# Second-layer logits on half of the array's rows for each of two heads, and output projections by 512 columns

## The chip, the cores and the metric

One core of one Trainium2 chip runs the whole kernel. Its engines are TensorE (PE in the profile, with PEld for its weight loads), VectorE (DVE), ScalarE (ACT), GpSimd (POOL) and SyncE (SP, which issues most DMAs). The metric is the device time of one execution in microseconds (us), as the median of several runs.

## The reference

A decoder trunk of two layers on a sequence of 1024 tokens with width 1024, in float32. Layer A is a gated DeltaNet layer; layer B is sliding-window attention with 32 query heads of 64 and four shared key and value heads. Both end with a projection by a weight of 2048 x 1024 that is added to the residual stream. The part that matters here:

```python
def swa_sink_mixer(h, w_in, q_gain, sinks, w_out, k_band, v_band, bias, mask):
    q, z = jnp.split(h @ w_in, 2, axis=-1)
    q = rms_norm(q.reshape(B, T, B_Q_HEADS, B_HD), q_gain) * (B_HD ** -0.5)
    q = q.reshape(B, nb, BLOCK, B_KV_HEADS, B_GROUP, B_HD)
    logits = jnp.einsum("bnqkgd,bnskd->bnkgqs", q, k_band).astype(jnp.float32) + bias
    ...
    o = jnp.einsum("bnkgqs,bnskd->bnqkgd", probs.astype(v_band.dtype), v_band)
    o = o.reshape(B, T, B_W) * jax.nn.silu(z)
    return o @ w_out          # and x = x + that, as at the end of layer A
```

A block is 128 queries, and its keys are the 128 of its own block and the 128 before them, so that each head's logits of a block are a 128 x 256 product over a depth of 64.

## The kernel before

Large products are taken at float32 precision by splitting each operand into a high part (rounded to the type fp32r, which TensorE takes in one pass) and a low part (the rest, again fp32r), and adding high x high, low x high and high x low in PSUM. Weights come in tiles of 128 x 1024 numbers: SP loads `wraw`, POOL or ACT makes `whi`, DVE makes `wlo` in two halves (`weight`, lines 138 to 158). TensorE's order is written out by hand: the code yields after small steps, and `interleave` lets a front stream of work go ahead by the numbers yielded while a back stream fills in. The other engines' instructions are put in order by a scheduler at build time.

*Output projections* (`out_proj`, called once for layer A with its weight `a_w_out` and once at the end for layer B with `b_w_out`). For each half of the tokens (512) and each half of the output columns (512), four PSUM banks `ps[c]`, one for each 128 tokens, collect 2048 rows of depth. `og_load` brings the layer's output in from HBM in four parts `k4` of 512 rows and splits them into `oh`, `ol`. A weight tile is 512 rows x 256 columns (`four` in `weights`): the loop over `b` takes the left and the right 256 columns, and each tile serves 4 x 4 x 3 = 48 matmuls with 256 moving columns. There are 32 such tiles in each projection, 3072 matmuls in both. The matmuls are lines 919 (`whi`, `oh`), 920 (`wlo`, `oh`) and 921 (`whi`, `ol`); line 925 adds the residual.

*Attention of layer B.* Eight groups of four heads (`groups`), eight blocks each: 64 blocks run through `b_attend`. For a block:

- `q_up` (lines 1137, 1139): POOL rounds the normalised queries to fp32r into `qh`, and DVE writes the low part beside it, so that a head has 64 high and 64 low numbers.
- `q_turn` (1146, 1149): TensorE transposes the four heads (fp32r, 128 x 128 each) into a PSUM tile `tp`, and ACT copies it to `qT`. Each head then fills all 128 rows of the array: high part above, low part below.
- `logits` (1166, 1167): for each head one matmul with the high keys `kh` and one with the low keys `kl`, 256 moving columns each. Both key tiles hold the 64 key rows twice, one above the other (`key_stack`). So a block has eight matmuls, four to each of two PSUM tiles `lg`. DVE then applies the mask (1168), adds the bias and takes the row maximum (1172); ACT does the exponentials (1182); POOL divides (1186).
- `turn` (1192): TensorE transposes the four heads' probabilities (float32), and ACT and DVE copy them out.
- `values` (1213): probabilities times values, two heads side by side on the left and right 64 columns of the array.

In each step of the loop of `b_attend` the calls are `turn(i)`, `q_turn(i + 3)` and `q_up(i + 4)`, `logits(i + 2)`, `values(i - 1)`, and between them the back stream computes the next queries (`gemm_tc`, lines 971 to 973, 256 columns) and gates (`gemm_ct`, lines 180, 182, 184, 512 columns).

Of the kernel before, what the change touches and what calls it, by code (L numbers as in the profile page):

```python
# [7 lines left out]
F32 = mybir.dt.float32  # L8
F32R = mybir.dt.float32r
# [9 lines left out]
P = 128  # L19
# [45 lines left out]
class Kernel:  # L65
# [831 lines left out]
    def out_proj(self, og, resid, cur, tiles, raws, px, acc, dst, finish):  # L897


        nc = self.nc  # L900
        for half in range(2):
            xs, nxt = [], []
            for cp in range(2):
                cs = slice(cp * 512, cp * 512 + 512)
                ps = [acc.tile([P, 2, 256], F32, name="acc") for _ in range(4)]
                for k4 in range(4):
                    oh, ol = cur[k4]
                    for b in range(2):
                        hi, lo = self.take()
                        if cp == 0 and (k4, b) == (2, 0):  # L910
                            self.flush()
                            for c in range(4):
                                xs.append(px.tile([P, D], F32, name="xo", bufs=4))
                                nc.sync.dma_start(xs[c], resid[half * 4 + c])
                        for c in range(4):
                            ts = slice(c * P, c * P + P)
                            po = ps[c][:, b, :]
                            for kk in range(4):
                                nc.tensor.matmul(po, oh[:, kk, ts], hi[:, kk, :], start=(k4 + kk + b == 0), stop=False)  # L919
                                nc.tensor.matmul(po, oh[:, kk, ts], lo[:, kk, :], start=False, stop=False)  # L920
                                nc.tensor.matmul(po, ol[:, kk, ts], hi[:, kk, :], start=False, stop=(k4 + kk + b == 7))  # L921
                                if kk % 2:
                                    self.tick()
                            if (k4, b) == (3, 1):
                                nc.vector.tensor_tensor(out=xs[c][:, cs], in0=ps[c].rearrange("p b c -> p (b c)"),
                                                        in1=xs[c][:, cs], op=ALU.add)
# [199 lines left out]
    def b_attend(self, groups):  # L1126

        nc, bp, sb, aps = self.nc, self.bp, self.sb, self.aps
        blocks = [(X, n) for X in groups for n in range(NB)]
        qh, qT, Ls, pTs = {}, {}, {}, {}  # L1130
# [11 lines left out]
        def q_turn(i):  # L1142
            t = qh.pop(i)
            ps = aps.tile([P, 4, P], F32R, name="tp", bufs=3)
            for e in range(4):
                nc.tensor.transpose(out=ps[:, e, :], in_=t[:, e, :, :].rearrange("p a d -> p (a d)"),
                                    identity=self.identr)
            qT[i] = bp.tile([P, 4, P], F32R, name="qT")
            nc.scalar.copy(out=qT[i], in_=self.f32(ps))

        def logits(i):

            X, n = blocks[i]
            kh, kl = X.keys
            sk = self.sink[:, 4 * X.hg:4 * X.hg + 4]
            q = qT.pop(i)
            k0 = 0 if n else P
            ksl = slice((n - 1) * P + k0, (n + 1) * P)
            L = Ls[i] = bp.tile([P, 4, P], F32, name="lsb", bufs=3)
            m = sb.tile([P, 4], F32, name="m")  # L1160
            two = [P, 2, P]
            for pr in range(2):
                ps = aps.tile([P, 2, 256], F32, name="lg")
                for j in range(2):
                    e = 2 * pr + j
                    nc.tensor.matmul(ps[:, j, k0:256], q[:, e, :], kh[:, ksl], start=True, stop=False)
                    nc.tensor.matmul(ps[:, j, k0:256], q[:, e, :], kl[:, ksl], start=False, stop=True)  # L1167
                nc.vector.copy_predicated(ps[:, :, P:256], self.up.bitcast(I32).unsqueeze(1).broadcast_to(two),
                                          ps[:, :, 0:P] if n else self.neg.unsqueeze(2).broadcast_to(two))
                for j in range(2):  # L1170
                    e = 2 * pr + j
                    nc.vector.tensor_tensor_reduce(out=L[:, e, :], in0=ps[:, j, P:256], in1=X.bias[:, e, :],
                                                   scale=1.0, scalar=sk[:, e:e + 1], op0=ALU.add, op1=ALU.max,
                                                   accum_out=m[:, e:e + 1])
            nm = sb.tile([P, 4], F32, name="nm")
# [41 lines left out]
                self.b_done(X)  # L1217

        last = len(blocks) - 1
        q_up(0)  # L1220
        q_up(1)
        q_turn(0)
        yield 1.0
        logits(0)
        q_turn(1)
        q_up(2)
        yield 1.5
        logits(1)
        q_turn(2)
        q_up(3)  # L1230
        yield 2.5
        fill = (1.2, 1.2, 0.6, 0.6, 1.2)
        steps = iter(())
        for i, (X, n) in enumerate(blocks):
            turn(i)
            yield fill[0]
            if i + 3 <= last:
                q_turn(i + 3)
            if i + 4 <= last:
                q_up(i + 4)  # L1240
            yield fill[1]
            if i + 2 <= last:
                logits(i + 2)
            yield fill[2]
            if X.hg < 7:
                nxt = groups[X.hg + 1]
                if n == 0:
                    nxt.keys, steps = self.key_stack(nxt.hg // 2) if X.hg % 2 else (X.keys, iter(()))
                    self.b_bias(nxt)
                next(steps, None)  # L1250
            yield fill[3]
            if i:
                values(i - 1)
            yield fill[4]
# [85 lines left out]
    def weights(self):  # L1340
# [15 lines left out]
                for b in (32 + 2 * i, 33 + 2 * i):  # L1356
                    yield col(self.win, b, None)
        for _ in range(2):
            for c in (0, 2):
                for k in range(4):  # L1360
                    for b in range(2):
                        yield four(rows("a_w_out"), k, c + b, None)
        wkv = I["w_kv"].rearrange("(k p) c -> p k c", p=P)
        for c in range(2):
            for k in range(2):
# [5 lines left out]
            else:  # L1371
                yield col(bin_, 16 + 2 * hg + j, self.gcolb[:, 8:16])
        for _ in range(2):
            for c in (0, 2):
                for k in range(4):
                    for b in range(2):
                        yield four(rows("b_w_out"), k, c + b, None)

    def dump(self, name, ap):
        self.nc.sync.dma_start(self.dbg[name], ap)  # L1380
# [21 lines left out]
```

## Time and profile before

| | us |
|---|---|
| median of 3 runs (1887.74 to 1893.08) | 1890.71 |
| the profiled execution | 1894.54 |
| its span, first to last instruction | 1892.8 |
| layer A up to its projection | 0 to 899.4 |
| layer A's projection (`out_proj`) | 899.4 to 1089.5 |
| keys, values, first queries | 1089.5 to 1167 |
| attention of layer B | 1167 to 1704.3 |
| layer B's projection (`out_proj`) | 1704.3 to 1892.8 |

TensorE is busy for 97% of the span, DVE for 65%, ACT for 44%, POOL for 27%. A matmul's duration in the profile is its latency from start to end; several are in the array at a time, so that the distance from one start to the next, not the duration, is what a matmul costs. A timeline row that ends in x8 stands for eight instructions of one line in a row; its duration runs from the first start to the last end.

### The profile page before, as it was taken

How to read it: one execution, taken by the hardware profiler on the slowest of the kernel's cores; microseconds unless marked ns; L12 is line 12 of the kernel's file. 1: busy time of each engine (PE TensorE's matmuls, PEld its weight loads, DVE VectorE, ACT ScalarE, POOL GpSimd, SP SyncE). 2: the span in 40 equal slices, each digit the busy share in tenths (PEclk: the TensorE clock that was granted, in tenths of full speed). 3: DMA queues.
4: the chain of work that ended last, by engine and by line, in shares of the span. 5: the costliest groups of instructions: out<-in, count | busy, mean ns of one | idle time of the engine just before them, and what ended most of it. 6: DMA issues, size and time to landing. Idle time of an engine off the chain costs nothing.

```text
span 1892.8 us, 34012 instructions
## 1 busy us (share of the span) xinstructions
PE 1829.7 (97%) x13186; PEld 1567.2 (83%) x13186; DVE 1239.6 (65%) x3014; ACT 838.1 (44%) x1968; POOL 512.6 (27%) x581
## 2 busy tenths in 40 slices
PE   6999999999999998999999999999999999999999
PEld 5667777787878776778999999888788788879999
DVE  6677776868595878765545366787776776753432
ACT  6446353635445364423011043656756666771100
POOL 0222222322232223221211232333433333321211
PEclk9999999999999999999999999999999999999999
DMA  4611111111111111133654321111211111226542
GB/s 149 143 37 34 56 45 57 34 56 46 34 57 34 46 34 58 33 96 99 229 182 152 112 90 46 42 38 46 67 32 48 56 49 43 73 73 200 188 166 82
DMA packets 151270, 149.74 MB, mean 79 GB/s; under 512 B 7242, under 2 KB 124484, under 8 KB 151108
## 3 DMA queue, kind: packets, MB, share of 16 engines
q1 hardware_dynamic: 140768, 130.40, 22.2%
q10 hardware_dynamic: 10340, 17.16, 2.9%
q8 instruction: 104, 1.70, 0.4%
q14 instruction: 58, 0.48, 0.1%
HBM read 116.05 MB, written 31.49 MB: 78 GB/s over the span
## 4 chain that ended last, share of the span: by engine, by line
PE 68%; DVE 13%; issue 5%; ACT 4%; POOL 3%; DMA 1%; POOLq 0%; ACTq 0%; SPq 0%; DVEq 0%
PE mm L182 8%; PE mm L180 8%; PE mm L184 8%; PE acc L920 6%; PE acc L919 6%; PE acc L921 6%; PE mm L971 4%; PE mm L973 3%; PE mm L972 3%; DVE acc L494 3%; PE pv L1213 2%; DVE wlo L157 2%; PE tp L1192 1%; PE kqp L666 1%; PE lg L1167 1%
## 5 line engine op out<-in xcount | busy, mean ns | idle before, releaser
L180 PE MATMUL mm<-hh,whi 128*128 128x512 f32 (+1 forms) x1040 | 427.2, 411 | 2.6 <-ACT hh L246 2.5
L182 PE MATMUL mm<-hl,whi 128*128 128x512 f32 (+1 forms) x1040 | 417.3, 401 | 1.6 <-DVE hl L247 1.5
L184 PE MATMUL mm<-hh,wlo 128*128 128x512 f32 (+1 forms) x1040 | 415.1, 399 | 0.0
L157 DVE TENSOR_TENSOR wlo<-wraw,whi 128x512 fp32r<-128x512 f32 x292 | 210.8, 749 | 239.4 <-POOL whi L150 214.0
L150 POOL TENSOR_SCALAR whi<-wraw 128x1024 fp32r<-128x1024 f32 x110 | 121.8, 1107 | 493.2 <-PE acc L921 248.3
L180 PEld LDWEIGHTS mm<-hh,whi 128*128 128x128 f32 x1040 | 197.5, 190 | 38.1 <-issue 4.6
L184 PEld LDWEIGHTS mm<-hh,wlo 128*128 128x128 f32 x1040 | 197.1, 190 | 36.0 <-issue 4.2
L182 PEld LDWEIGHTS mm<-hl,whi 128*128 128x128 f32 x1040 | 197.5, 190 | 34.6 <-issue 4.2
L971 PE MATMUL mm<-whi,hh 128*128 128x256 f32 x608 | 179.9, 296 | 0.0
L494 DVE SCALAR_TENSOR_TENSOR acc<-u,cw,acc 128x512 f32<-128x512 f32 x192 | 160.8, 839 | 23.5 <-POOL acc L491 21.0
L973 PE MATMUL mm<-whi,hl 128*128 128x256 f32 x608 | 171.8, 283 | 0.0
L972 PE MATMUL mm<-wlo,hh 128*128 128x256 f32 x608 | 171.7, 282 | 0.0
L919 PE MATMUL acc<-whi,hh 128*128 128x256 f32 x512 | 145.0, 283 | 0.0
L920 PE MATMUL acc<-wlo,hh 128*128 128x256 f32 x512 | 144.9, 283 | 0.0
L921 PE MATMUL acc<-whi,hl 128*128 128x256 f32 x512 | 144.9, 283 | 0.0
L971 PEld LDWEIGHTS mm<-whi,hh 128*128 128x128 f32 x608 | 115.6, 190 | 10.9 <-issue 10.8
L1182 ACT ACTIVATE lsb<-lsb,nm 128x128 f32<-128x128 f32 x256 | 99.8, 392 | 54.6 <-DVE se L1178 44.4
L972 PEld LDWEIGHTS mm<-wlo,hh 128*128 128x128 f32 x608 | 115.8, 190 | 0.2
L973 PEld LDWEIGHTS mm<-whi,hl 128*128 128x128 f32 x608 | 115.5, 190 | 0.0
L920 PE MATMUL acc<-wlo,oh 128*128 128x256 f32 x384 | 108.7, 283 | 1.2 <-DVE wlo L157 1.2
L919 PE MATMUL acc<-whi,oh 128*128 128x256 f32 x384 | 108.6, 283 | 0.0
L921 PE MATMUL acc<-whi,ol 128*128 128x256 f32 x384 | 108.5, 283 | 0.0
(355 smaller groups left out, 4207.0 us busy)
## 6 DMA issues: line engine op xcount, KB each, us to landing
wraw<-in_a_w_in SPq DMA_DIRECT2D x48, 512.0 KB, 4.0
wraw<-in_a_w_out SPq DMA_DIRECT2D x32, 512.0 KB, 4.2
wraw<-in_b_w_in SPq DMA_DIRECT2D x32, 512.0 KB, 4.0
wraw<-in_b_w_out SPq DMA_DIRECT2D x32, 512.0 KB, 3.9
og<-zs SPq DMA_DIRECT2D x32, 256.0 KB, 2.0
ogT<-zs SPq DMA_DIRECT2D x24, 256.0 KB, 2.1
btab<-lt SPq DMA_DIRECT2D x1, 4096.0 KB, 24.2
dm<-gd SPq DMA_DIRECT2D x8, 512.0 KB, 3.7
```

What stands on the lines that cost most here:

```text
L150: nc.gpsimd.tensor_scalar(out=hi, in0=raw, scalar1=1.0, scalar2=1.0, op0=ALU.mult, op1=ALU.mult)
L157: nc.vector.tensor_tensor(out=lo[:, ks], in0=raw[:, ks], in1=self.f32(hi[:, ks]), op=ALU.subtract)
L180: nc.tensor.matmul(ps, hi[:, k, :], hh[:, k, :], start=(k == 0), stop=False)
L182: nc.tensor.matmul(ps, hi[:, k, :], hl[:, k, :], start=False, stop=False)
L184: nc.tensor.matmul(ps, lo[:, k, :], hh[:, k, :], start=False, stop=(k == KT - 1))
L494: nc.vector.scalar_tensor_tensor(out=acc, in0=u[:, t:t + 512], scalar=cw[:, t, blk:blk + 1], in1=acc, op0=ALU.mult, op1=ALU.add)
L919: nc.tensor.matmul(po, oh[:, kk, ts], hi[:, kk, :], start=(k4 + kk + b == 0), stop=False)
L920: nc.tensor.matmul(po, oh[:, kk, ts], lo[:, kk, :], start=False, stop=False)
L921: nc.tensor.matmul(po, ol[:, kk, ts], hi[:, kk, :], start=False, stop=(k4 + kk + b == 7))
L971: nc.tensor.matmul(ps, hh[:, k, ts], hi[:, k % 4, :], start=(k == 0), stop=False)
L972: nc.tensor.matmul(ps, hh[:, k, ts], lo[:, k % 4, :], start=False, stop=False)
L973: nc.tensor.matmul(ps, hl[:, k, ts], hi[:, k % 4, :], start=False, stop=(k == KT - 1))
```

## The change

It has three parts.

- *Projections.* A weight tile is now 256 rows x 512 columns. It serves 4 x 2 x 3 = 24 matmuls with 512 moving columns. The 32 tiles of a projection, their size and their order of use by depth stay; only the split between rows and columns of a tile is another.
- *Queries.* `q_up` is gone. `q_turn` transposes the float32 queries directly, two heads at a time (64 + 64 numbers make one 128 x 128 transpose, two transposes for a block). ACT rounds the PSUM tile to the high part, and DVE subtracts that from the PSUM tile for the low part.
- *Logits.* A head's 64 numbers now lie either in the upper or the lower 64 rows of the array (`a` = 0 or 1). Each pair of heads takes three passes (high x high, low x high, high x low), and in each pass the two heads' matmuls stand next to each other, one on either half of the rows, each with its own PSUM tile. A block has twelve matmuls with 64 rows in place of eight with 128.

```diff
@@ out_proj
-                ps = [acc.tile([P, 2, 256], F32, name="acc") for _ in range(4)]
+                ps = [acc.tile([P, 512], F32, name="acc") for _ in range(4)]
...
-                            po = ps[c][:, b, :]
-                            for kk in range(4):
-                                nc.tensor.matmul(po, oh[:, kk, ts], hi[:, kk, :], start=(k4 + kk + b == 0), stop=False)
-                                nc.tensor.matmul(po, oh[:, kk, ts], lo[:, kk, :], start=False, stop=False)
-                                nc.tensor.matmul(po, ol[:, kk, ts], hi[:, kk, :], start=False, stop=(k4 + kk + b == 7))
-                                if kk % 2:
-                                    self.tick()
+                            for kk in range(2):
+                                k = 2 * b + kk
+                                nc.tensor.matmul(ps[c], oh[:, k, ts], hi[:, kk, :], start=(k4 + k == 0), stop=False)
+                                nc.tensor.matmul(ps[c], oh[:, k, ts], lo[:, kk, :], start=False, stop=False)
+                                nc.tensor.matmul(ps[c], ol[:, k, ts], hi[:, kk, :], start=False, stop=(k4 + k == 6))
+                                self.tick()
@@ b_attend
-        def q_up(i):
-            X, n = blocks[i]
-            qv = X.q[n // 4]
-            c = n % 4
-            t = qh[i] = bp.tile([P, 4, 2, 64], F32R, name="qh")
-            nc.gpsimd.tensor_scalar(out=t[:, :, 0, :], in0=qv[:, c, :, :], scalar1=1.0, scalar2=1.0,
-                                    op0=ALU.mult, op1=ALU.mult)
-            nc.vector.tensor_tensor(out=t[:, :, 1, :], in0=qv[:, c, :, :], in1=self.f32(t[:, :, 0, :]),
-                                    op=ALU.subtract)
-
         def q_turn(i):
-            t = qh.pop(i)
-            ps = aps.tile([P, 4, P], F32R, name="tp", bufs=3)
-            for e in range(4):
-                nc.tensor.transpose(out=ps[:, e, :], in_=t[:, e, :, :].rearrange("p a d -> p (a d)"),
-                                    identity=self.identr)
-            qT[i] = bp.tile([P, 4, P], F32R, name="qT")
-            nc.scalar.copy(out=qT[i], in_=self.f32(ps))
+            X, n = blocks[i]
+            qv = X.q[n // 4][:, n % 4, :, :].rearrange("p (r a) d -> p r (a d)", a=2)
+            ps = aps.tile([P, 4, P], F32, name="tp", bufs=3)[:, 0:2, :]
+            for pr in range(2):
+                nc.tensor.transpose(out=ps[:, pr, :], in_=qv[:, pr, :], identity=self.ident)
+            hi = bp.tile([P, 2, P], F32R, name="qT")
+            lo = bp.tile([P, 2, P], F32R, name="qTl")
+            nc.scalar.copy(out=hi, in_=ps)
+            nc.vector.tensor_tensor(out=lo, in0=ps, in1=self.f32(hi), op=ALU.subtract)
+            qT[i] = hi, lo
...
+            pss = [aps.tile([P, 2, 256], F32, name="lg") for _ in range(2)]
             for pr in range(2):
-                ps = aps.tile([P, 2, 256], F32, name="lg")
-                for j in range(2):
-                    e = 2 * pr + j
-                    nc.tensor.matmul(ps[:, j, k0:256], q[:, e, :], kh[:, ksl], start=True, stop=False)
-                    nc.tensor.matmul(ps[:, j, k0:256], q[:, e, :], kl[:, ksl], start=False, stop=True)
+                for w, k in ((qh, kh), (ql, kh), (qh, kl)):
+                    for a in range(2):
+                        rs = slice(64 * a, 64 * a + 64)
+                        nc.tensor.matmul(pss[a][:, pr, k0:256], w[rs, pr, :], k[rs, ksl], start=(w is qh and k is kh),
+                                         stop=(k is kl))
+            for a in range(2):
+                ps = pss[a]
                 nc.vector.copy_predicated(...)
@@ weights (both projections)
-            for c in (0, 2):
-                for k in range(4):
-                    for b in range(2):
-                        yield four(rows("a_w_out"), k, c + b, None)
+            for c in (0, 512):
+                for k in range(0, 16, 2):
+                    yield rows("a_w_out")[:, k:k + 2, c:c + 512], [2, 512], None
```

Two places show how this stands in the engines' queues. The first is TensorE at the logits of a block in the middle of the attention stage; `lg` is the logits' PSUM tile, `mm` that of the back stream. Before:

```order
L971 MATMUL mm<-whi,hh_85 128x256
L972 MATMUL mm<-wlo,hh_85 128x256
L973 MATMUL mm<-whi,hl_86 128x256
L1166 MATMUL lg<-kh,qT 128x256
L1167 MATMUL lg<-kl,qT 128x256
```

After, at such a place:

```order
L180 MATMUL mm<-hh_87,whi 128x512
L182 MATMUL mm<-hl_88,whi 128x512
L184 MATMUL mm<-hh_87,wlo 128x512
L1159 MATMUL lg<-kh,qT 128x256 x2
L1159 MATMUL lg<-kh,qTl 128x256 x2
L1159 MATMUL lg<-kl,qT 128x256 x2
```

Before, the pair of rows 1166 and 1167 stands four times; now the group of three rows, each of them two matmuls (upper and lower half), stands twice. Back-stream matmuls on the full array stand ahead of and behind the group in both.

The second place is DVE around a block's mask step; `tp` is the PSUM tile of transposes, `pT` the probabilities, `ssqb` the queries' sums of squares. Before:

```order
L1200 TENSOR_TENSOR pT_15268<-tp,cst 128x512
L1139 TENSOR_TENSOR qh<-qr,qh 128x4x64
L1098 TENSOR_REDUCE ssqb<-sq 128x8
L1168 COPY_PREDICATED lg<-cst,lg 128x2x128 x2
L1172 ISA lsb,m<-lg,bias,sink 128x128
L1172 ISA m 128x1
```

After, at such a place:

```order
L1195 TENSOR_TENSOR pT_14833<-tp,cst 128x512
L1139 TENSOR_TENSOR qTl<-tp,qT 128x256
L1179 TENSOR_TENSOR den<-den,se 128x4
L1180 RECIPROCAL den<-den 128x4
L1163 COPY_PREDICATED lg<-cst,lg 128x2x128 x2
L1167 ISA lsb,m<-lg,bias,sink 128x128
L1167 ISA m 128x1
```

The subtraction that made the low queries from SBUF, ahead of the transposes and behind POOL, now reads the PSUM tile, behind the transposes and ACT; it keeps its place between the probabilities' copy and the next mask step.

## Rows read from the trace of the kernel before

**Rows 1.** Stretches: length, busy (count) of PE, PEld, DVE, ACT, POOL, clock, DMA.

```profile
899.40:1089.50 190.10, 188.20 (x1571) 187.79 (x1570) 86.04 (x123) 24.12 (x32) 41.16 (x37) 1.00 0.51 168
1167.00:1704.30 537.30, 529.54 (x3630) 443.51 (x3629) 386.57 (x1392) 351.59 (x947) 188.31 (x235) 0.99 0.17 52
1704.30:1892.80 188.50, 184.72 (x1540) 184.36 (x1536) 68.31 (x91) 14.02 (x15) 32.59 (x30) 1.00 0.49 159
```

**Rows 2.** Waits of PE, layer B's attention, then layer A's projection: total us, times, longest.

```profile
PE tp L1192 <- POOL lsb L1186: 5.9, 5, 2.0
...
PE acc L920 <- DVE wlo L157: 1.9, 2, 1.2
```

**Rows 3.** A stretch inside layer B's projection, PE alone: length, busy (count), clock, DMA.

```profile
1720.00:1820.00 100.00, 100.00 (x836) 1.00 0.57 187
```

**Rows 4.** Timeline of PE, an uninterrupted run of 512-column matmuls (start us, duration us).

```profile
605.76 0.39 PE L180 MATMUL mm<-hh,whi 128*128 128x512 f32 x1
...
615.05 0.39 PE L184 MATMUL mm<-hh,wlo 128*128 128x512 f32 x1
```

**Rows 5.** Timeline of PE, query transposes and logits of one block.

```profile
1401.62 0.46 PE L1146 MATMUL tp<-identr,qh 128*128 128x128 f32 x4
1401.92 0.47 PE L180 MATMUL mm<-hh,whi 128*128 128x512 f32 x1
1402.22 0.40 PE L182 MATMUL mm<-hl,whi 128*128 128x512 f32 x1
...
1403.38 0.28 PE L1166 MATMUL lg<-kh,qT 128*128 128x256 f32 x1
...
1404.34 0.40 PE L180 MATMUL mm<-hh,whi 128*128 128x512 f32 x1
```

**Rows 6.** Timeline of PE, the float32 transposes of a block's probabilities.

```profile
1408.52 0.60 PE L1192 MATMUL tp<-cst,lsb 128*128 128x128 f32 x4
1408.87 0.47 PE L184 MATMUL mm<-hh,wlo 128*128 128x512 f32 x1
1409.18 0.39 PE L180 MATMUL mm<-hh,whi 128*128 128x512 f32 x1
```

**Rows 7.** Timeline of PE in layer A, 64 x 64 products amid full-array matmuls.

```profile
743.33 1.15 PE L687 MATMUL kqp<-w 64*64 64x64 f32 x32
744.41 0.50 PE L182 MATMUL mm<-hl,whi 128*128 128x512 f32 x1
...
746.45 0.63 PE L756 MATMUL kqp<-cst,xt 64*64 64x64 f32 x8
747.02 0.50 PE L180 MATMUL mm<-hh,whi 128*128 128x512 f32 x1
...
747.59 0.40 PE L184 MATMUL mm<-hh,wlo 128*128 128x512 f32 x1
747.91 1.14 PE L761 MATMUL kqp<-w,lt 64*64 64x64 f32 x16
748.99 0.50 PE L180 MATMUL mm<-hh,whi 128*128 128x512 f32 x1
749.32 0.39 PE L182 MATMUL mm<-hl,whi 128*128 128x512 f32 x1
```

**Rows 8.** Timeline of PE, transposes on 32 rows and all 128 columns.

```profile
59.88 0.68 PE L382 MATMUL tr<-cst,zs 32*128 32x32 f32 x8
60.49 0.50 PE L180 MATMUL mm<-hh,whi 128*128 128x512 f32 x1
60.82 0.39 PE L182 MATMUL mm<-hl,whi 128*128 128x512 f32 x1
```

**Rows 9.** Timeline of PE, logits of a first block, 128 moving columns.

```profile
1428.80 0.27 PE L1167 MATMUL lg<-kl,qT 128*128 128x128 f32 x1
...
1429.58 0.44 PE L180 MATMUL mm<-hh,whi 128*128 128x512 f32 x1
```

**Rows 10.** DMA issues of the page: count, KB each, us to landing.

```profile
wraw<-in_a_w_out SPq DMA_DIRECT2D x32, 512.0 KB, 4.2
```

More of the change, by code (lines that the diff above doesn't have):

```diff
@@ L1129, in b_attend, with q_turn @@
         blocks = [(X, n) for X in groups for n in range(NB)]
-        qh, qT, Ls, pTs = {}, {}, {}, {}
-        def q_up(i):
+        qT, Ls, pTs = {}, {}, {}
+        def q_turn(i):
             X, n = blocks[i]
-            qv = X.q[n // 4]
-            c = n % 4
-            t = qh[i] = bp.tile([P, 4, 2, 64], F32R, name="qh")
-            nc.gpsimd.tensor_scalar(out=t[:, :, 0, :], in0=qv[:, c, :, :], scalar1=1.0, scalar2=1.0,
-                                    op0=ALU.mult, op1=ALU.mult)
-            nc.vector.tensor_tensor(out=t[:, :, 1, :], in0=qv[:, c, :, :], in1=self.f32(t[:, :, 0, :]),
-                                    op=ALU.subtract)
-        def q_turn(i):
-            t = qh.pop(i)
-            ps = aps.tile([P, 4, P], F32R, name="tp", bufs=3)
-            for e in range(4):
-                nc.tensor.transpose(out=ps[:, e, :], in_=t[:, e, :, :].rearrange("p a d -> p (a d)"),
-                                    identity=self.identr)
-            qT[i] = bp.tile([P, 4, P], F32R, name="qT")
-            nc.scalar.copy(out=qT[i], in_=self.f32(ps))
+            qv = X.q[n // 4][:, n % 4, :, :].rearrange("p (r a) d -> p r (a d)", a=2)
[7 more added lines that the diff above has]
+            qT[i] = hi, lo
         def logits(i):
@@ L1155, in logits @@
             sk = self.sink[:, 4 * X.hg:4 * X.hg + 4]
-            q = qT.pop(i)
+            qh, ql = qT.pop(i)
             k0 = 0 if n else P
@@ L1161, in logits @@
             two = [P, 2, P]
+            pss = [aps.tile([P, 2, 256], F32, name="lg") for _ in range(2)]
             for pr in range(2):
-                ps = aps.tile([P, 2, 256], F32, name="lg")
-                for j in range(2):
-                    e = 2 * pr + j
-                    nc.tensor.matmul(ps[:, j, k0:256], q[:, e, :], kh[:, ksl], start=True, stop=False)
-                    nc.tensor.matmul(ps[:, j, k0:256], q[:, e, :], kl[:, ksl], start=False, stop=True)
+                for w, k in ((qh, kh), (ql, kh), (qh, kl)):
[5 more added lines that the diff above has]
+                ps = pss[a]
                 nc.vector.copy_predicated(ps[:, :, P:256], self.up.bitcast(I32).unsqueeze(1).broadcast_to(two),
                                           ps[:, :, 0:P] if n else self.neg.unsqueeze(2).broadcast_to(two))
-                for j in range(2):
-                    e = 2 * pr + j
-                    nc.vector.tensor_tensor_reduce(out=L[:, e, :], in0=ps[:, j, P:256], in1=X.bias[:, e, :],
+                for pr in range(2):
+                    e = 2 * pr + a
+                    nc.vector.tensor_tensor_reduce(out=L[:, e, :], in0=ps[:, pr, P:256], in1=X.bias[:, e, :],
                                                    scale=1.0, scalar=sk[:, e:e + 1], op0=ALU.add, op1=ALU.max,
@@ L1219, in b_attend @@
         last = len(blocks) - 1
-        q_up(0)
-        q_up(1)
         q_turn(0)
@@ L1225, in b_attend @@
         q_turn(1)
-        q_up(2)
         yield 1.5
@@ L1229, in b_attend @@
         q_turn(2)
-        q_up(3)
         yield 2.5
@@ L1238, in b_attend @@
                 q_turn(i + 3)
-            if i + 4 <= last:
-                q_up(i + 4)
             yield fill[1]
@@ L1373, in weights @@
         for _ in range(2):
[L1374 to L1377, printed above, removed]
+            for c in (0, 512):
+                for k in range(0, 16, 2):
+                    yield rows("b_w_out")[:, k:k + 2, c:c + 512], [2, 512], None
     def dump(self, name, ap):
```

3 lines of the change are left out of this document (1 added, 2 removed).

## The prediction

> **What bounds the kernel now.** I read the stretches first. In both projections TensorE is busy for 98% of the time or more, while DVE, ACT and POOL are far below half; in the attention stage it is busy for 529.5 of 537.3 us, DVE for 386.6 [rows 1]. The list of TensorE's waits comes next: in the attention stage the longest item is 5.9 us, transposes that wait for POOL's division; the other items are smaller; in layer A's projection it waited 1.9 us for a low weight half [rows 2]. So in all three stages that the change touches, TensorE's queue sets the time, and what counts there is the distance between starts, since a duration is latency. The sum is therefore made of start distances on TensorE, against the profiled execution's 1894.54 us; that lies 0.2% above the median of the runs, 1890.71 us, so I apply the difference in us to the median.
>
> **Projections.** With 256 moving columns, 100 us of the stage hold 836 matmuls, some two of which only reach in: 0.120 us each [rows 3]. With 512 columns, an undisturbed run has 41 distances between 605.76 and 615.05: 0.2266 us [rows 4]. Amid other work the same matmul takes 0.232 us (five from 1402.22 to 1403.38) [rows 5]. A weight tile thus goes from 48 x 0.120 = 5.76 us to 24 x 0.2266 = 5.44 us, 0.32 us less; at 0.232 it would be 5.57, 0.19 less. The projections are long undisturbed runs like the one of rows 4, so I take that. Layer A's projection begins on data that is just arriving, and its wait for a low weight half shows that [rows 2]; for its first four tiles I count no gain. That leaves 60 of 64 tiles: 60 x 0.32 = **19.2 us less**; the small end is 60 x 0.19 = 11.4 us.
>
> The rows say that a matmul costs its columns plus some 13 ns: 2 x 0.120 - 0.2266 [rows 3, 4]. The Trainium skill (TensorE: Matmul & The Clock Gate, section Back-to-back issue gap) gives a fixed part of 2.5 ns for each matmul. By that the 1536 matmuls that disappear would bring 3.8 us; the trace decides against it, but this is a rival below.
>
> Cover: a weight tile lands 4.2 us after its issue [rows 10], two raw buffers alternate, and POOL and DVE are busy for 17% and 36% of the last stage [rows 1]. The same 32 tiles a projection come 6% more often, which this hides. If that cover went, each late tile would cost what it is late, as in rows 2 (0.9 us on average).
>
> **Query transposes.** Four fp32r transposes and the next matmul go from 1401.62 to 1402.22; less the 0.23 us of that 512-column matmul, 0.37 us [rows 5]. Four float32 transposes: 1408.52 to 1409.18 less 0.23, 0.43 us, or 0.108 each [rows 6]. The new `q_turn` has two of the latter, 0.22 us. 64 blocks x (0.37 - 0.22) = **9.6 us less**. All 64 stand on the path, because the queue is full on either side.
>
> **Logits.** Now: eight matmuls from 1403.38 to 1404.34, 0.96 us [rows 5]. Afterwards twelve half-row matmuls, and three questions.
>
> First, do the two halves run at once? No row shows upper and lower rows with all 128 columns. The nearest do it with quarters: line 687 alternates between the upper left and the lower right quarter, line 761 uses one quarter; 32 of the former take the 1.08 us of 16 of the latter [rows 7]. I take side by side, six pairs at the 0.120 us of one matmul of 256 columns: 0.72 us. If each of the two also paid its own 13 ns, a pair would take 0.133 us, 0.80 in all; one after another, 1.44.
>
> Second, what does leaving the full array cost? Around line 761: the matmul before it has 0.32 us (747.59 to 747.91) where 0.23 is usual, 0.09 more; the one behind it 0.33 (748.99 to 749.32), 0.10 more. The body: 16 take 1.08 us, the 8 of line 756 take 0.57, so 0.064 for one more and 0.06 for none. Together 0.25 us for each excursion [rows 7]. On 32 rows with all 128 columns, the shape nearest to the new one: 0.61 us for eight is 0.10 above 8 x 0.064, and 0.33 behind them is 0.10 above 0.23; with the 0.09 ahead, 0.29 [rows 8].
>
> The Trainium skill (TensorEngine Tiling (Array Packing), section Key Properties) says the same in words, that changing the tiling mode drains TensorE; it speaks against this change, since its section Theoretical Speedup promises up to twice for a depth of 64. Without the drain, logits would be 0.72 us and not 1.08: that is a rival too.
>
> Third, the first weight load after the switch is not hidden. In a first block, where only 128 columns move, seven distances take 0.78 us, 0.111 each [rows 9], against the 0.064 of rows 7: a full fp32r load is some 0.05 us longer, which may count once or twice. So the excursion costs 0.25 to 0.39; I take 0.36, from 0.29 plus about 0.07, the row-strip being the nearest form. Logits: 0.72 + 0.36 = 1.08 us, 0.12 more than now; 64 x 0.12 = **7.7 us more**. Ends: 0.72 + 0.25 = 0.97 (0.6 us more in all), 0.80 + 0.39 = 1.19 (14.7 us more). I count the eight first blocks like the rest; their loads set 0.111 now as then.
>
> **Other engines.** POOL loses an operation for each block, ACT's copy halves from 512 to 256 columns a row, DVE's subtraction keeps its 256 columns and only changes its source to PSUM. All three are well below TensorE in this stage [rows 1], so I cost this at nothing. The new wait: DVE's low part stands behind TensorE's transposes and ACT's copy; queued behind it are the next block's mask steps, which free the `lg` tiles that the block after that needs. The code turns a block's queries one full step (537.3 / 64 = 8.4 us) before its logits, so what is late by a microsecond isn't seen. POOL's division, on which the 5.9 us hang, has one thing less ahead of it. I leave the waits as they are, with 6 us less and 3 us more as ends.
>
> **The sum.** -19.2 - 9.6 + 7.7 = -21.1 us: 1873.4 for the profiled execution, 1890.7 - 21.1 = **1870 us** for the median. The likeliest case's own ends: -19.2 - 9.6 + 0.6 - 6 = -34 (1857) and -11.4 - 9.6 + 14.7 + 3 = -3 (1887); all at one end together is unlikely.
>
> **Rivals.**
>
> *The halves run one after another* (or their weight loads do), on the slower side. For it: no row with 64 rows by 128 columns and fp32r, and both halves write all 128 partitions of PSUM. Against it: the quarters of rows 7, and the two halves have a PSUM tile each. Then logits take 1.44 + 0.36 = 1.80 us, 0.84 more: +53.8 - 28.8 = +25, 1916 us. It decides from a pair distance of (0.96 + 28.8/64 - 0.36)/6 = 0.175 us on: above that the kernel is slower. Chance 0.10.
>
> *New waits take the gain of the attention stage and more.* Five waits for POOL now cost 5.9 us, 1.2 each [rows 2]; if DVE, behind TensorE and ACT twice a block, made two more such in each of eight groups, that is +19 us: 1889 us, no change. Against it: 150 us of idle DVE in the stage [rows 1]. Chance 0.08.
>
> *The wide matmul brings nothing in the projections.* If a 512-column matmul costs nearly twice a 256-column one there, 3.8 us are left of 19.2: -3.8 - 9.6 + 7.7, about 1885 us. (The Trainium skill's 2.5 ns on TensorE: Matmul & The Clock Gate, Back-to-back issue gap, would do just this.) Against it: rows 4. Chance 0.04.
>
> *No price for the half rows.* Logits 0.72 us: 64 x 0.24 = 15.4 less, so -19.2 - 9.6 - 15.4 = -44: 1847 us. Against it: rows 8, where a strip of rows paid. Chance 0.04.
>
> **How the numbers follow.** The forecast holds the remaining 0.74. Range 1860 to 1888: it takes in the forecast's bounds but for the most extreme corner, and the waits of the second and third rival up to 1888; left out are 1916, 1847, and the corner, under 2 in 10. A measurement tells about 0.3% (5.7 us) from no change, so faster means under 1885.0. Faster: 0.74 x 0.97 + 0.04 + half of 0.04 + a quarter of 0.08, 0.80. Slower: 0.10 and a little of the waits, 0.11. Same: 0.09.
>
> **What would show it.** In the timeline of the changed kernel, 512-column projection matmuls 0.227 us apart and each tile 5.44 us; two query transposes 0.22 us; logits' starts in close pairs, pairs 0.12 us apart, from first logits to the next full matmul about 0.9 us and a longer distance on either side. Pairs that are 0.2 us or more apart, a list of waits with DVE or ACT items of over 10 us in the attention stage, or projections at 0.235 a matmul would make the prediction wrong.

## The result and the profile after

The changed kernel takes **1872.72 us** (median of 4 runs, 1872.09 to 1873.68), the kernel before 1891.89 us beside it (4 runs, 1887.74 to 1893.26). The ratio is 0.9903, with an interval of 0.9886 to 0.9920. The profiled execution took 1872.77 us with a span of 1870.7 us, 22.1 us less than the span before.

The stretches of the kernel after (length, busy time and count of PE, PEld, DVE, ACT, POOL, granted clock, DMA share, GB/s), which answer to [rows 1], start at layer A's projection, at the first logits and at layer B's projection:

```profile
898.30:1080.90 182.60, 181.85 (x803) 147.26 (x802) 86.36 (x123) 24.38 (x32) 40.89 (x37) 1.00 0.52 174
1160.20:1692.50 532.30, 528.03 (x3755) 422.26 (x3754) 382.92 (x1394) 341.99 (x947) 160.22 (x174) 0.99 0.17 53
1692.50:1870.70 178.20, 174.43 (x770) 144.06 (x768) 67.31 (x91) 14.33 (x15) 31.44 (x30) 1.00 0.50 167
```

Layer A's projection is 7.5 us shorter (190.1 to 182.6), layer B's 10.3 us (188.5 to 178.2), and the attention stage, from its first logits on, 4.6 us (536.9 to 532.3). Layer A ahead of its projection took 1.2 us less with the same code (in the profiles of all runs it lies between 896.7 and 900.8 us), and the stretch between that projection and the first logits 1.3 us more.

Not all of this is the change. Two of the experiments below keep the projections of the kernel before; there layer A's takes 188.7 us, as in this row of the kernel with the attention stage alone:

```profile
897.50:1086.20 188.70, 188.00 (x1571) 187.79 (x1569) 86.14 (x123) 24.45 (x32) 40.56 (x37) 1.00 0.50 169
```

The 1.5 us more in the profile before are one tile, the fifth: it took 7.21 us with a wait of 1.2 us for its low weight half, and 5.75 in those two. So 6.0 of the 7.5 us belong to the change. The attention stage of the kernel before took 534.5 us in the kernel with the projections alone, and the changed one 533.5 us in the kernel with the attention stage alone: by these profiles the gain there lies between 1 and 4.6 us. TensorE still fills all three stages, so distances between starts are again the thing to read.

TensorE's timeline of the kernel after in the attention stage: query transposes, and further on the logits of one block (start us, duration us; x2 is two matmuls of one line in a row):

```profile
1386.38 0.38 PE L1135 MATMUL tp<-cst,qr 128*128 128x128 f32 x2
1386.52 0.37 PE L969 MATMUL mm<-whi,hh 128*128 128x256 f32 x1
1386.72 0.28 PE L970 MATMUL mm<-wlo,hh 128*128 128x256 f32 x1
...
1387.90 0.28 PE L971 MATMUL mm<-whi,hl 128*128 128x256 f32 x1
1388.11 0.38 PE L1159 MATMUL lg<-kh,qT 64*128 64x256 f32 x2
1388.33 0.28 PE L1159 MATMUL lg<-kh,qTl 64*128 64x256 f32 x2
1388.45 0.28 PE L1159 MATMUL lg<-kl,qT 64*128 64x256 f32 x2
...
1388.80 0.28 PE L1159 MATMUL lg<-kl,qT 64*128 64x256 f32 x2
1389.01 0.39 PE L969 MATMUL mm<-whi,hh 128*128 128x256 f32 x1
1389.23 0.28 PE L970 MATMUL mm<-wlo,hh 128*128 128x256 f32 x1
```

The transposes of [rows 5] took 0.37 us; here 1386.38 to 1386.72 is 0.34, less the 0.12 of the matmul in between 0.22 us. The logits stand in six pairs. The two of a pair start 3 to 5 ns apart, and pairs follow each other after 0.118 us. Leaving the full array and coming back is called an excursion here. It is visible in four distances: into the pairs 0.21 us (0.09 over the usual 0.12), behind the first pair 0.22 (0.10 over), out of them 0.21 (0.09 over), and behind the first full matmul 0.22 (0.10 over). Together 0.38 us. In each half the first weight load starts 1 to 2 ns ahead of its matmul, later ones 0.11 to 0.12 us ahead, so the first is not hidden. From L971 ahead of the logits to the second full matmul behind them, less those two matmuls' own 0.12 each, a block's median is 1.10 us; the same reading of the kernel before gives 0.95.

Starts of the first matmul of successive weight tiles in layer A's projection, then in layer B's, kernel after:

```profile
955.07 0.40 PE L919 MATMUL acc<-whi,oh 128*128 128x512 f32 x1
960.55 0.40 PE L919 MATMUL acc<-whi,oh 128*128 128x512 f32 x1
966.17 0.39 PE L919 MATMUL acc<-whi,oh 128*128 128x512 f32 x1
971.77 0.40 PE L919 MATMUL acc<-whi,oh 128*128 128x512 f32 x1
...
1741.65 0.39 PE L919 MATMUL acc<-whi,hh 128*128 128x512 f32 x1
1747.09 0.39 PE L919 MATMUL acc<-whi,hh 128*128 128x512 f32 x1
```

In layer B every tile takes 5.44 us but the first (5.59). In layer A undisturbed tiles take 5.48, 5.62 and 5.60 in turn, 5.57 on average. Before, an undisturbed tile took 5.75 or 5.76 in either.

The waits of TensorE in the attention stage, which answer to the first row of [rows 2] (total us, times, longest):

```profile
PE lg L1159 <- DVE m L1167: 3.2, 2, 1.7
PE tp L1187 <- POOL lsb L1181: 1.0, 2, 0.7
```

The wait for POOL's division fell from 5.9 to 1.0 us, and the one for DVE's mask steps grew from 0.6 to 3.2 us; its two parts lie in the first 7 us of the stage.

### The profile page after: what moved, and what is told of

The parts are those of the page before. It is cut to its first block, busy times and chain, and to the rows that moved or that the text cites. A ratio compares the mean times of both kernels' runs of the same rounds, so it can differ in the third digit from the quotient of the medians.

```text
span 1870.7 us, 31174 instructions
## 1 busy us (share of the span) xinstructions
PE 1812.2 (97%) x11778; PEld 1466.2 (78%) x11778; DVE 1233.6 (66%) x3014; ACT 829.1 (44%) x1970; POOL 482.0 (26%) x517
## 3 DMA queue, kind: packets, MB, share of 16 engines
q1 hardware_dynamic: 124384, 130.40, 22.5%
## 4 chain that ended last, share of the span: by engine, by line
PE 75%; DVE 10%; issue 4%; POOL 3%; ACT 2%; DMA 0%; POOLq 0%; ACTq 0%; DVEq 0%; SPq 0%
PE mm L182 9%; PE mm L180 9%; PE mm L184 9%; PE acc L920 6%; PE acc L921 6%; PE acc L919 6%; PE mm L969 4%; PE mm L970 4%; PE mm L971 4%; PE pv L1208 3%; PE lg L1159 3%; DVE acc L494 3%; PE tp L1187 1%; DVE wlo L157 1%; PE sc L793 1%
## 5 line engine op out<-in xcount | busy, mean ns | idle before, releaser
L971 PE MATMUL mm<-whi,hl 128*128 128x256 f32 x608 | 171.8, 283 | 0.0
L1181 POOL TENSOR_TENSOR lsb<-lsb,den 128x512 f32<-128x512 f32 x64 | 67.8, 1059 | 196.3 <-DVE den L1180 152.4
L971 PEld LDWEIGHTS mm<-whi,hl 128*128 128x128 f32 x608 | 115.7, 190 | 0.0
L153 POOL TENSOR_TENSOR wraw<-wraw,gcolb 128x512 f32<-128x512 f32 x72 | 81.0, 1146 | 130.9 <-DMA wraw<-in_b_w_in 44.1
L491 POOL TENSOR_SCALAR acc<-u,cw 128x512 f32<-128x512 f32 x64 | 56.4, 880 | 182.8 <-ACT u L487 169.1
L919 PE MATMUL acc<-whi,hh 128*128 128x512 f32 x256 | 99.7, 390 | 0.0
L921 PE MATMUL acc<-whi,hl 128*128 128x512 f32 x256 | 99.6, 389 | 0.0
L920 PE MATMUL acc<-wlo,hh 128*128 128x512 f32 x256 | 99.6, 389 | 0.0
```

The source lines that it names most:

```text
L919: nc.tensor.matmul(ps[c], oh[:, k, ts], hi[:, kk, :], start=(k4 + k == 0), stop=False)
L920: nc.tensor.matmul(ps[c], oh[:, k, ts], lo[:, kk, :], start=False, stop=False)
L921: nc.tensor.matmul(ps[c], ol[:, k, ts], hi[:, kk, :], start=False, stop=(k4 + k == 6))
L971: nc.tensor.matmul(ps, hl[:, k, ts], hi[:, k % 4, :], start=False, stop=(k == KT - 1))
```

## The experiments

### The projections alone

The kernel before with the first part of the change only (the hunks `out_proj` and `weights` of the diff).

> Only the first part of the change: weight tiles of 256 rows x 512 columns in both projections; queries and logits as before. Theory: a tile costs 5.44 us in layer B's projection and about 5.57 in layer A's, as in the changed kernel, in place of 5.76; with that 7.5 to 9 us go from layer A's projection and 10.2 from layer B's, 17.5 to 19 us in all, so about 1873.5. Rival: the projections gain only because the attention stage hands them data and queues in another state, or the attention stage carries half of the gain; then this kernel gains 10 us or less.

Measured: 1874.18 us (4 runs), the kernel before 1892.88 us (15 runs), ratio 0.9900 (0.9886 to 0.9913), 18.7 us less. The two projections bring nearly all of the gain, as expected. The whole change has the ratio 0.9903 (0.9886 to 0.9920): what the attention part adds on top of the projections is too small for these runs to tell.

### The attention stage alone

The other two parts of the change: the changed kernel with the projections of the kernel before.

> Only the second part: queries transposed in pairs in float32 and logits on half rows in three passes; projections by 256 columns as before. Theory: transposes -9.3 us, logits +9.8 us (1.10 us a block with the way in and out, where it was 0.95), and TensorE's waits in the attention stage 3 to 4 us less; so 3 to 5 us faster, about 1888, on the edge of what can be told from no change. Rival: half rows pay by themselves (0.72 us of streaming in place of 0.96), which would be 15 us and 1876; or the waits come back and it is no faster at all.

Measured: 1889.15 us (11 runs) against 1892.88, ratio 0.9984 (0.9974 to 0.9994): 1 to 5 us less, 3.7 by the medians. Small, as expected, but not nothing. TensorE's waits for POOL's division are 1.4 us here, against 5.2 us in the kernel with the projections alone, so that these waits go with the attention part.

### Six on the upper half, then six on the lower half

```diff
-            for pr in range(2):
-                for w, k in ((qh, kh), (ql, kh), (qh, kl)):
-                    for a in range(2):
-                        rs = slice(64 * a, 64 * a + 64)
+            for a in range(2):
+                rs = slice(64 * a, 64 * a + 64)
+                for pr in range(2):
+                    for w, k in ((qh, kh), (ql, kh), (qh, kl)):
```

> The changed kernel, but a block's six matmuls on the upper rows all stand ahead of its six on the lower rows. Same matmuls, same operands. Theory: halves run at once only where they stand next to each other in TensorE's order, so 11 start distances of 0.117 us take the place of 6: about 0.58 us a block, 64 x 0.58 = +37 us, about 1910. Rival: the queue brings the second half forward by itself, or the halves never really overlapped and the trace's start times mislead; then nothing changes.

Measured: 1891.09 us in one profiled run, 18 us over the changed kernel; the attention stage alone is 20.9 us longer (553.3 against 532.3). That is neither 37 nor 0. TensorE's timeline shows why (logits of one block of this kernel):

```profile
1385.04 0.28 PE L971 MATMUL mm<-whi,hl 128*128 128x256 f32 x1
1385.26 0.38 PE L1159 MATMUL lg<-kh,qT 64*128 64x256 f32 x1
1385.48 0.28 PE L1159 MATMUL lg<-kh,qTl 64*128 64x256 f32 x1
1385.60 0.28 PE L1159 MATMUL lg<-kl,qT 64*128 64x256 f32 x1
1385.60 0.39 PE L1159 MATMUL lg<-kh,qT 64*128 64x256 f32 x2
1385.83 0.29 PE L1159 MATMUL lg<-kh,qTl 64*128 64x256 f32 x2
1385.94 0.29 PE L1159 MATMUL lg<-kl,qT 64*128 64x256 f32 x2
1386.06 0.28 PE L1159 MATMUL lg<-kh,qT 64*128 64x256 f32 x1
1386.18 0.28 PE L1159 MATMUL lg<-kh,qTl 64*128 64x256 f32 x1
1386.30 0.28 PE L1159 MATMUL lg<-kl,qT 64*128 64x256 f32 x1
1386.51 0.38 PE L969 MATMUL mm<-whi,hh 128*128 128x256 f32 x1
```

Six matmuls share three places and six stand alone: nine places of 0.118 us in place of six, 0.35 us more, and a block's median is indeed 1.44 us against 1.10; 64 x 0.34 is 22 us. The row x2 at 1385.60 holds two matmuls of high keys and high queries, the first of the lower half (the seventh in the program) and the fourth of the upper half. The first of the two starts 7 ns behind the third (kl,qT at 1385.60) and the other 0.11 us later; in the timelines above, matmuls on one half are 0.11 us or more apart, so the early one is the seventh, beside the third. The fourth then stands alone, and the eighth and ninth start with the fifth and sixth (the x2 rows at 1385.83 and 1385.94). The lower half's first distance, 1385.60 to 1385.83, is as long as the upper half's, 1385.26 to 1385.48. So the halves do work at the same time, and a matmul for the idle half goes ahead of some that wait for the busy one, but only of a few: the seventh went ahead of three, and not of four by starting with the second. The expectation's mistake was to think that only neighbours can share a place.

The Trainium skill (TensorE: Matmul & The Clock Gate, section The mechanism) says that matmuls start strictly in program order, with only weight loads pulled ahead. This trace differs: the seventh starts at 1385.60 and the fifth not before 1385.83. The measurement decides.

### Three on the upper half, then three on the lower half

```diff
             for pr in range(2):
-                for w, k in ((qh, kh), (ql, kh), (qh, kl)):
-                    for a in range(2):
-                        rs = slice(64 * a, 64 * a + 64)
+                for a in range(2):
+                    rs = slice(64 * a, 64 * a + 64)
+                    for w, k in ((qh, kh), (ql, kh), (qh, kl)):
```

> The changed kernel with another order of a block's twelve logits: for each pair of heads three matmuls on the upper 64 rows, then three on the lower 64 rows, where the changed kernel alternates one and one. The same matmuls and the same results. Theory (lookahead): a matmul of the lower half may start while those issued up to three places ahead of it wait for the upper half. In the kernel with six and six, the seventh starts 5 ns behind the fourth and ahead of the fifth and sixth, and a block's logits have nine distances, not eleven. With three and three each lower matmul is three places behind its partner, so all pair up but for what the reach leaves: six distances of 0.116 us or one more, 0 to 0.12 us for a block, 0 to +7.4 us against 1870.7 of span. Rival: only neighbours in the queue start together. Then a block has nine to eleven distances, 0.35 to 0.58 us more for a block, +22 to +37 us.

Measured: 1874.68 us in one profiled run, attention stage 533.4 us against 532.3. The timeline of one block:

```profile
1389.47 0.39 PE L1159 MATMUL lg<-kh,qT 64*128 64x256 f32 x2
1389.69 0.29 PE L1159 MATMUL lg<-kh,qTl 64*128 64x256 f32 x2
```

The order of starts is again one pair after another, though the program has three and three; the two of a pair now start 10 ns apart, and a block takes 1.11 us against 1.10. That only neighbours pair up is excluded, and a reach of three places fits both kernels. (The expectation has the seventh of six and six beside the fourth; the trace has it beside the third, as above.) Only these two orders were run, so that three is a general limit is not shown.

### Two excursions for a block

```diff
             for pr in range(2):
+                if pr:
+                    yield 0.6
                 for w, k in ((qh, kh), (ql, kh), (qh, kl)):
...
             if i + 2 <= last:
-                logits(i + 2)
-            yield fill[2]
+                yield from logits(i + 2)
+            else:
+                yield fill[2]
...
```

The 0.6 that the loop yielded behind a block's logits (`fill[2]`) is now yielded between its two pairs of heads. There the back stream puts full-array matmuls, so that 62 blocks leave the full array once more.

> The changed kernel, with a block's logits split: the first pair of heads, then full-array matmuls of the back stream, then the second pair. The same work, with some 62 more ways off the full array and back. Theory: one way in and out costs 0.36 to 0.40 us, so 62 x 0.36 to 0.40 = +22 to +25 us, about 1896. Rival: what costs is the passes themselves (three in place of two), and the way in and out is hidden by the queue; then under 5 us more.

Measured: 1900.19 us in one profiled run, 27 us over the changed kernel. One of the two excursions of a block:

```profile
1391.47 0.28 PE L971 MATMUL mm<-whi,hl 128*128 128x256 f32 x1
1391.68 0.38 PE L1161 MATMUL lg<-kh,qT 64*128 64x256 f32 x2
1391.90 0.28 PE L1161 MATMUL lg<-kh,qTl 64*128 64x256 f32 x2
1392.02 0.28 PE L1161 MATMUL lg<-kl,qT 64*128 64x256 f32 x2
1392.23 0.39 PE L969 MATMUL mm<-whi,hh 128*128 128x256 f32 x1
1392.45 0.27 PE L970 MATMUL mm<-wlo,hh 128*128 128x256 f32 x1
```

The same four long distances stand around three pairs as around six. Read in the same manner, such an excursion takes 0.74 us, so two of them 1.48 against the one of 1.10: 0.38 us for the second. 62 x 0.38 = 23.6; the attention stage grew by 22.5 (554.9 against 532.3). The rest of the 27 is elsewhere: the third tile of layer B's projection took 9.46 us in place of 5.44, with a late low weight half. So the price of an excursion is measured, and it is the same with three pairs in it as with six. The Trainium skill (TensorEngine Tiling (Array Packing), section Key Properties) says that a change of the tiling mode drains TensorE; the runs fit that, with 0.38 us there and back.

### Values right behind the logits

The products of probabilities and values use half of the columns, so they are an excursion of their own. Here the two stand together, with no full-array matmul between them.

```diff
             if i + 2 <= last:
                 logits(i + 2)
+            if i:
+                values(i - 1)
...
-            if i:
-                values(i - 1)
             yield fill[4]
```

> The changed kernel, with the products with the values moved ahead so that they directly follow a block's logits: 61 times the queue goes from half rows to half columns without full-array matmuls between. Theory: each change of shape costs a drain of 0.09 us and an exposed weight load, and one change falls away for each block, 0.15 to 0.24 us; so 9 to 15 us less than the changed kernel, 1858 to 1864. Rival: the price is paid for each group of other shape, whatever stands beside it (half rows to half columns costs as much as the way back to the full array and in again); then it stays at 1872.

Measured: **1865.5 us** (4 runs, 1863.6 to 1867.99), ratio to the kernel before 0.9856 (0.9843 to 0.9870). This interval lies wholly below that of the changed kernel; the profiled spans are 6.8 us apart (1863.9 and 1870.7). It is faster than both kernels. TensorE around one block:

```profile
1383.81 0.28 PE L971 MATMUL mm<-whi,hl 128*128 128x256 f32 x1
1384.02 0.39 PE L1159 MATMUL lg<-kh,qT 64*128 64x256 f32 x2
...
1384.72 0.28 PE L1159 MATMUL lg<-kl,qT 64*128 64x256 f32 x2
1384.93 1.08 PE L1208 MATMUL pv<-pT,vv 128*64 128x256 f32 x8
1385.95 0.39 PE L969 MATMUL mm<-whi,hh 128*128 128x256 f32 x1
```

And the longest of its waits in the attention stage:

```profile
PE tp L1187 <- POOL lsb L1181: 4.0, 3, 2.4
```

Going from half rows to half columns costs the same 0.21 us as going to the full array (1384.72 to 1384.93), so three switches are left of four. In the changed kernel logits and values take 1.10 and 1.21 us of their own, here 2.12 together: 0.19 less. For 61 times that is some 11.6 us; 3.0 us of it goes back as longer waits for POOL (4.0 against 1.0). The attention stage is 7.6 us shorter, at 524.8 us. That is below the 9 to 15 expected: of the 4.0 us missing from 11.6, these waits are 3.0, and 1 us is not traced.

### The weights of layer A's projection in one pool

Layer A's projection takes its weight halves in turn from two pools, `wsp` twice and an extra one (`wx`) once; layer B's takes all from `wsp`. The tiles of 5.48 us are those in `wx`.

```diff
-                    self.wpools, self.wcount, self.depth = [self.wsp, wx, self.wsp], 1, 2
+                    self.wpools, self.wcount, self.depth = [self.wsp], 0, 1
```

> The changed kernel, but layer A's projection takes all its weight tiles from the two buffers that lie below 45 KB of a partition, none from the one at 131 KB, two tiles being in flight in place of three. Theory: a 512-column matmul costs 0.227 us or 0.231 to 0.238 depending on where its two operands lie, near one another or far apart, and all 32 tiles of layer A's projection then take the 5.61 us that two of three take now: 11 x 0.13 = 1.4 us more in that stage. Rival: every third tile is fast for another reason, such as the rhythm in which tiles are made; then tiles of 5.48 us are still there.

Measured: 1875.11 us in one profiled run, span 1873.3 against 1870.7. First matmuls of successive tiles in layer A's projection:

```profile
958.09 0.39 PE L919 MATMUL acc<-whi,oh 128*128 128x512 f32 x1
963.69 0.39 PE L919 MATMUL acc<-whi,oh 128*128 128x512 f32 x1
969.29 0.39 PE L919 MATMUL acc<-whi,oh 128*128 128x512 f32 x1
```

TensorE's wait for a low weight half in that projection, 0.7 us in the changed kernel:

```profile
PE acc L920 <- DVE wlo L157: 2.3, 1, 2.3
```

Every undisturbed tile now takes 5.60 us and the rhythm of three is gone, as expected; a wait of 2.3 us near the start comes on top. So it is the buffers, not the rhythm in which tiles are made, that set 5.48 or 5.60. The edit also leaves one tile less in flight, but layer B's projection has as few, at 5.44 us. It is not the pool by itself either: layer B reads the same `wsp`, with the layer's output (`hh`, `hl`) in other buffers. What in a pair of buffers costs 4 to 11 ns a matmul stays open. The tiles before the change showed nothing of it.

### Whose work made the waits for POOL's division

First, the kernel before with the rounding of the queries on ACT in place of POOL:

```diff
-            nc.gpsimd.tensor_scalar(out=t[:, :, 0, :], in0=qv[:, c, :, :], scalar1=1.0, scalar2=1.0,
-                                    op0=ALU.mult, op1=ALU.mult)
+            nc.scalar.copy(out=t[:, :, 0, :], in_=qv[:, c, :, :])
```

> The kernel before, with the rounding of the queries to their high part on ACT in place of POOL; nothing else. Theory: TensorE's waits for POOL's division (5.9 us in five waits) hang on POOL's queue, in which the rounding stands ahead of the division and itself waits; without it they fall to about 1 us as in the changed kernel, so 3 to 5 us less, 1887 to 1889. Rival: the waits come from the late weights for which POOL waits, or from ACT and DVE ahead of the division; then no change, or slower, since ACT has 0.4 us a block more.

Measured: 1893.2 us (11 runs) against 1890.72 (15 runs), ratio 1.0011 (1.0002 to 1.0020). No gain (by the interval 0.4 to 4 us more), and the wait is still there, 6.4 us. Second, the changed kernel with POOL's rounding put back, into a tile that nobody reads:

```diff
+        def q_up(i):
+            X, n = blocks[i]
+            t = bp.tile([P, 4, 64], F32R, name="qh")
+            nc.gpsimd.tensor_scalar(out=t, in0=X.q[n // 4][:, n % 4, :, :], scalar1=1.0, scalar2=1.0,
+                                    op0=ALU.mult, op1=ALU.mult)
...
+            if i + 4 <= last:
+                q_up(i + 4)
```

> The changed kernel with one more operation on POOL for each block, where the kernel before had its rounding of the queries: 256 numbers a row, from the normalised queries to a tile that nobody reads. Theory: the kernel before lost 5.9 us to POOL's division because the rounding stood ahead of it on POOL's queue; then TensorE's wait for the division in the attention stage comes back from 1.0 to 4 us or more, and the span grows by 3 to 5 us over 1870.7. Rival, which the kernel with the rounding on ACT speaks for (its wait was 6.4 us without the rounding on POOL): what went is DVE's low part, which waited for POOL ahead of the mask steps, or mere pacing; then the wait stays below 2 us and the span within 2 us.

Measured: 1869.92 us in one profiled run, span 1867.9. TensorE's wait for the division in the attention stage, with the rounding on ACT:

```profile
PE tp L1191 <- POOL lsb L1185: 6.4, 3, 3.4
```

The same with POOL's rounding put back into the changed kernel:

```profile
PE tp L1193 <- POOL lsb L1187: 0.4, 1, 0.4
```

DVE's wait for the high part of the queries in that stage, in the kernel before:

```profile
DVE qh L1139 <- POOL qh L1137: 39.7, 40, 3.4
```

In the kernel with the rounding on ACT:

```profile
DVE qh L1138 <- ACT qh L1137: 10.4, 14, 2.0
```

And in the kernel after:

```profile
DVE qTl L1139 <- ACT qT L1138: 9.5, 14, 2.0
```

POOL's additional operation costs nothing (0.4 us of waits, the attention stage at 532.6 us against 532.3), so its load wasn't the cause. One thing the run does not bring back: in the kernel before, POOL's rounding stood 68.4 us in all behind TensorE's transposes, which read the buffer that it writes, and a tile that nobody reads has no such wait. What did change is DVE: in the kernel before, its low part stood 39.7 us in all in front of POOL's rounding, and the mask steps behind it in the queue; now its wait is 9.5. That this shortened the waits for the division is likely but not shown: with the rounding on ACT, DVE's wait also fell, to 10.4, yet the division's wait stayed, with ACT's exponentials behind one more operation. No run separates the two.

## Why the prediction was right, step by step

The forecast was 1870 us, 21 less; measured are 1872.7 us and, by the ratio, 15 to 22 less (18.4 by its middle).

- **Projections, -19.2.** The two stretches are 17.8 us shorter in the profiles, of which 1.5 us are the one late tile of the profile before: -16.3 by the change. The kernel with this part alone is 18.7 us faster, with an interval of 16.5 to 21.6. Layer B's is the forecast to 0.1 us: 32 tiles at 5.44. In layer A the step "the projections are long undisturbed runs like the one of rows 4, so I take that" was wrong by size: a tile takes 5.57 on average, 0.19 less than before. That is the small end that I had worked out, though for another reason (other work); the run with one pool points to the buffers. Leaving out the first four tiles was too cautious: the first two, disturbed before and after, went from 5.84 to 5.68 and from 6.71 to 6.49 us, and gained as much as the others. (DVE is busy for 45% of layer A's projection, not "far below half"; nothing hung on that.)
- **Query transposes, -9.6.** Read block by block 0.365 to 0.220 us, 9.3 us less.
- **Logits, +7.7.** 0.95 to 1.10 us, 0.15 in place of 0.12 a block: +9.7. Both of the unknown parts came out nearly as taken: pairs side by side at 0.118 (taken 0.12), and 0.38 for the excursion (taken 0.36). The first rival, halves one after another, is out: pairs start together, and even in the kernel that issues six and six half of the lower ones share a place. The fourth, no price for half rows, is out by the price of a second excursion, 0.38 us.
- **Waits, 0.** They fell: TensorE's for POOL from 5.9 to 1.0 us, against 1.7 more at the logits (3.2 now; before, two waits of 0.9 and 0.6). Together 3.2 us less, inside the ends of -6 and +3. The second rival's waits for DVE showed only as this growth in the first blocks, not as two in each group. I had weighed what DVE's low part would wait for behind TensorE and ACT and not what it had waited for before, the 39.7 us behind POOL in the list of DVE's waits.
- **The third rival**, that a matmul of 512 columns costs twice one of 256, is out: 5.44 and 5.57 us a tile against 5.76.

By these, the attention stage is -9.3 + 9.7 - 3.2 = -2.8, measured -4.6 between the two profiles and -1 to -5 in the timed kernel with this part alone.

So the mechanism was right, and that the sum came so close is partly luck: the projections gave 2.9 us less than forecast and the logits cost 2.0 more, while the waits, taken at nothing, gave 3.2 back.

One thing lies outside the steps. Between layer A's projection and the first logits 1.3 us came on top. Three microseconds of the kernel after, behind two waits of TensorE for DVE (0.69 and 1.14 us), in the columns of the first fence:

```profile
1090.60:1093.60 3.00, 3.00 (x15) 3.00 (x16) 0.82 (x2) 0.66 (x2) 0.00 (x0) 0.50 0.02 5
```

The same place in the kernel with the projections alone, behind waits of 0.67 and 1.14 us:

```profile
1088.90:1091.90 3.00, 3.00 (x26) 3.00 (x27) 1.59 (x3) 1.72 (x4) 0.00 (x0) 1.00 0.02 5
```

At 0.50, which is 1.2 GHz, 15 matmuls went through in place of 26. The kernel with the projections alone runs the same code there at 1.00, and so do four of the changed kernel's variants, with 77.6 to 77.9 us for the stretch against 79.2. These 1.5 us belong to an execution and not to the change.

## What to carry to other kernels

Where TensorE sets the time, count distances between starts. Here 256 columns took 0.120 us and 512 took 0.227, so that 13 ns of each matmul do not depend on its columns; in a stretch where TensorE waits for nothing the wider moving operand wins. Half-row matmuls in pairs are worth their price only if much is done in one excursion, since leaving the full array cost 0.38 us with three pairs as with six; put work of different partial shapes side by side. Before crediting a stage's gain to a change, read the same stage in other runs of the same code: here that took 1.5 us off. Before costing a moved operation's new wait, read the old one in the waits of its own engine.

## What the runs showed of the hardware

- Two matmuls on opposite halves of the rows start 3 to 5 ns apart and share 0.118 us. Issued three places apart they still do (10 ns); issued six apart, half of them do, and a matmul starts ahead of three that stand before it in the program.
- A 512-column matmul takes 0.227 us in layer B's projection and 0.227 or 0.231 to 0.238 in layer A's, by the buffers that it reads, as far as the run with one pool tells; with 256 columns these buffers made no difference (5.75 to 5.76 us a tile).
- Half rows to half columns costs as much at the entry (0.21 us to the next start) as half rows to the full array.
- Two waits of 0.7 and 1.1 us were in one execution followed by 3 us at half the clock, and in another, with waits of the same length, not.
